# A two-block transformer on one core: triangle solved from a transposed copy, inverse decay by a second scan, squares summed by contiguous additions, 14 ring slots through the attentions

## The chip, the cores and the metric

One core of a Trainium2 chip runs the whole program. The metric is device time of one execution in microseconds. TensorE (PE in the profile) does matrix products, VectorE (DVE) and ScalarE (ACT) the elementwise work, GpSimd (POOL) little, and SyncE (SP) issues nearly all DMAs.

## The reference, cut to what matters

256 tokens of width 1024 go through two blocks, in float32.

```python
def first_block(x, mem, ...):                      # two layers
    for layer in range(2):
        att = (spatial gating if layer == 0 else dilated attention) + memory attention, projected
        x = layer_norm(ALPHA * x + att, ...)
        expert, gate = route(h, w_router, b_router)         # top 2 of 16 experts
        ffn = moe_ffn(h, expert, gate, w_gate, w_up, w_down)  # 16 x 3 matrices of 1024 x 1024
        x = layer_norm(ALPHA * x + ffn, ...)

def second_block(x, ...):                          # two layers
    for l in range(2):
        x = x + 0.5 * swiglu(rms_norm(x, norm_ffa[l]), ...)   # 1024 -> 2 x 2816 -> 1024
        x = x + hybrid_mixer(rms_norm(x, norm_mix[l]), ...)   # retention, sparse attention, rwkv7
        x = x + 0.5 * swiglu(rms_norm(x, norm_ffb[l]), ...)
    return rms_norm(x, norm_final)

def rms_norm(x, g):
    return x * rsqrt(mean(x * x, -1) + 1e-6) * g

def rwkv7_time_mix(...):                           # 8 heads of width 64, a state per head
    def step(S, inp):
        sa = einsum(S, -kk_t)
        S = S * w_t + sa * (kk_t * a_t) + v_t * k_t
        return S, einsum(S, r_t)
```

## The kernel before

**First block.** Weights come from HBM in tiles of 1 MB through a ring of slots in SBUF. In an attention (`attn_a`, `attn_b`) each unit of weights takes a ring slot (`raw_unit`), and ACT and DVE split it into a high and a low float32r part (`split_act`, L331 and L332, into the tiles `whi` and `wlo`), from which `mm3` makes three float32r matmuls for one float32 product (L100). A ring slot is free once its unit is split. The order of the DMAs on SP's queue is the program's; the expert weights of the following `moe` come right behind the last unit of the attention, so they begin to fill the ring while the attention still computes. In `moe` the eight pairs of experts each take 24 tiles (8 of `w_gate`, 8 of `w_up`, 8 of `w_down`), multiplied as plain float32 at L1870. `fetch` (issued at L1749) gives each tile a slot in turn: `slots = e.ring + 3` = 15, 12 of them in the ring and three in a pool `wst2` that exists in `moe` alone; tiles 11 to 15 have places of their own. From then on a fetch waits until TensorE has used what was in its slot. Before the sixth pair's third product there is a conditional branch (an overflow path, not taken), ahead of which `slots` tiles are fetched.

**Second block.** An FFN (`ffn`) streams weights in 512 KB tiles, split by ACT (L228) and DVE (L230), and does 11 column blocks of gate and up products with the down product of the block before in between. `rms_row` makes the factor of the norm: ACT squares x in two halves (L282), DVE sums each half over four strips of 256 with a reduction whose inner step is 256 elements (L283), adds the two (L284), a float32 matmul with ones sums over partitions (L286), then a root and a reciprocal (L289). It runs six times, within the first column block of an FFN or at the start of a mixer.

**Mixer.** The products of all branches are streams of L100 matmuls; the branches' own work is put between them by a priority. `rwkv_front` makes per group of two heads (`scaled`, four times) the decay: an exponential on ACT (L716), a running product over chunks of 32 by a scan on DVE (L718), and its inverse by a reciprocal (L721). `rwkv_back` then inverts the 128 unit triangles of 32 x 32 by forward substitution: they come back from DRAM into `LX`, one triangle in each partition, row by row; step t multiplies `X[:, :, :t+1]` by column t of the triangle (L811) and reduces (L812). The result goes through DRAM (`xscr`) into another layout, and the recurrence over chunks follows (`masks`, `solve`, `chunks`, `step`).

```python
    LXv = LX.rearrange("p (s t) -> p s t", s=32)
    for t in range(1, 32):
        nc.vector.tensor_mul(tmp, X[:, :, :t + 1], bc(LXv[:, :t + 1, t], 1, 16))
        nc.vector.tensor_reduce(X[:, :, t], tmp, axis=AX.X, op=OP.add)
```

`LXv[:, :t + 1, t]` is a column: its elements lie 32 floats (128 bytes) apart.

Of the kernel before, what the change touches and what calls it, by code (L numbers as in the profile page):

```python
# [111 lines left out]
def setup(ctx, tc, I, off):  # L112
    e = Env()
    e.tc, e.nc, e.I, e.off = tc, tc.nc, I, off
    nc = tc.nc
    P = lambda n, b, **k: ctx.enter_context(tc.tile_pool(name=n, bufs=b, **k))
    e.pool = P
    e.k = P("consts", 1)
    ident = e.k.tile([128, 128], F32, name="ident")
    nc.gpsimd.dma_start(ident, I["cst"][:, :128])  # L120
    e.c = {"ident": ident}
    e.ones = e.k.tile([128, 128], F32, name="ones")
    nc.vector.memset(e.ones, 1.0)
    e.eps = P("edge", 1, side="right").tile([128, 56], F32, name="eps")[:, :4]
    for i, v in enumerate((1e-6, 64e-5, 1e-5, -0.5 * E05)):
        nc.vector.memset(e.eps[:, i:i + 1], v)
    e.ahead, e.chain = 20000, 8000
    e.tail, e.first = (), None
    return e
# [145 lines left out]
def rms_row(e, cols=False, bank=None):  # L275

    nc = e.nc
    s1 = e.t1()
    part = [e.t1(), e.t1()]
    for i in range(2):  # L280
        sq = e.t4()
        nc.scalar.activation(sq.rearrange("p (k t) -> p k t", k=4), e.xT[:, 4 * i:4 * i + 4], AF.Square)  # L282
        nc.vector.tensor_reduce(part[i], sq.rearrange("p (k t) -> p t k", k=4), axis=AX.X, op=OP.add)  # L283
    nc.vector.tensor_add(s1, part[0], part[1])  # L284
    pb = (bank or e.bank)()
    nc.tensor.matmul(pb[:, :T], e.ones, s1, start=True, stop=True)  # L286
    rs = e.t1()
# [15 lines left out]
def turned(pool, n, name, o=TURN, tag=None):  # L303

    return pool.tile([128, n + 64], F32R, name=name, tag=tag or name)[:, o:o + n]


# [365 lines left out]
def rwkv_front(e, l, sub):  # L673
# [32 lines left out]
    def scaled(P):  # L706
# [9 lines left out]
        nc.scalar.activation(dsc[:, :, 1:33], c8(sig), AF.Exp, bias=e.eps[:, 3:4], scale=-0.5 * E05)  # L716
        W = e.t1(264).rearrange("p (c t) -> p c t", c=8)
        nc.vector.tensor_tensor_scan(W.rearrange("p c t -> p (c t)"), dsc.rearrange("p c t -> p (c t)"),  # L718
                                     e.c["scan1"], 0.0, OP.mult, OP.add)
        Wi = c8(sig)  # L720
        nc.vector.reciprocal(Wi, W[:, :, 1:33])  # L721
        WC = e.act.tile([128, 8], F32, name="WC", bufs=4)
# [71 lines left out]
def rwkv_back(e, l, front):  # L794
# [8 lines left out]
    for hf in range(2):  # L803
        nc.sync.dma_start(LX[hf * 64:(hf + 1) * 64], ltf)
    nc.vector.memset(LX[:, 0:1024:33], 1.0)
    LXv = LX.rearrange("p (s t) -> p s t", s=32)
    X = e.t2().rearrange("p (s t) -> p s t", s=16)
    nc.sync.dma_start(X, I["dec"][:, 2048:].rearrange("p (s t) -> p s t", s=16))
    for t in range(1, 32):
        tmp = e.t2().rearrange("p (s t) -> p s t", s=16)[:, :, :t + 1]  # L810
        nc.vector.tensor_mul(tmp, X[:, :, :t + 1], bc(LXv[:, :t + 1, t], 1, 16))  # L811
        nc.vector.tensor_reduce(X[:, :, t], tmp, axis=AX.X, op=OP.add)  # L812
# [269 lines left out]
def setup1(ctx, e):  # L1082
    nc = e.nc
    P = lambda n, b: ctx.enter_context(e.tc.tile_pool(name=n, bufs=b, reuse_waits="tile"))
    e.ring = 12
    e.wst = P("wst1", e.ring)
# [82 lines left out]

def split_unit(e, w, moving=False):  # L1170

    out = []
    for i in range(4):
        hi, lo = [turned(p, 512, n, 32 if moving else 0).rearrange("p (a b) -> p a b", a=2)
                  for p, n in ((e.whl, "whi"), (e.wlo, "wlo"))]
        split_act(e, w[:, 2 * i:2 * i + 2], hi, lo)
        out += [(hi[:, k], lo[:, k]) for k in range(2)]
    return out


def unit(e, src, moving=False):
    with e.tc.high_priority(offset=e.ahead):
        w = raw_unit(e, src.shape[1])
        load(e, w, src, 0, 1)
        return split_unit(e, w, moving)


def split_T(e, src, pool, wsrc):

    hh, hl = [turned(pool, KD * T, n).rearrange("p (k t) -> p k t", k=KD) for n in ("hh", "hl")]  # L1190
    sv = src.rearrange("(k p) t -> p k t", p=128)
# [164 lines left out]
def out_proj(e, w, parts):  # L1356
# [4 lines left out]
    for i, (k0, a) in enumerate(parts):  # L1361
# [6 lines left out]
        with e.tc.high_priority(offset=e.ahead):  # L1368
            w = raw_unit(e, 2)
            load(e, w, wv[:, k0:k0 + 2], 0, 1)  # L1370
            for j, n in jn:
                u[j, n] = [turned(p, 512, nm, 32) for p, nm in ((e.whl, "whi"), (e.wlo, "wlo"))]
                split_act(e, w[:, j, n * 512:(n + 1) * 512], *u[j, n])
# [13 lines left out]
def attn_a(e):  # L1387
# [17 lines left out]
    mem_keys(e, proj_T(e, u, mT))  # L1405
    nc.scalar.copy(e.mv, proj_N(e, unit(e, w8("w_mem_v", 0), True), mT))
    mp.close()
# [6 lines left out]
    for c in range(3):  # L1414
        pb = proj_N(e, unit(e, wv[:, :, 768 + c * 256:768 + (c + 1) * 256], True), hT)
        if c == 1:
# [50 lines left out]
def attn_b(e):  # L1467
# [17 lines left out]
    pool = hp.enter_context(e.tc.tile_pool(name="hT", bufs=1, side="right", reuse_waits="tile"))  # L1485
    hh, hl = [turned(pool, KD * T, n).rearrange("p (k t) -> p k t", k=KD) for n in ("hh", "hl")]

# [103 lines left out]
    for c in range(3):  # L1591
        sl = slice(c * 256, (c + 1) * 256)
        nc.scalar.copy(V[:, :, sl], proj_N(e, unit(e, wv[:, :, sl], True), hT))
    hp.close()
# [117 lines left out]
def moe(e, l, done, kv):  # L1712
# [11 lines left out]
    with ExitStack() as xs:  # L1724
        xT = xs.enter_context(tc.tile_pool(name="rx", bufs=1, reuse_waits="tile")).tile([128, KD, T], F32, name="xT")

        def evac(q, pt):
# [6 lines left out]
             for x in (2 * pr, 2 * pr + 1)]  # L1734
    loaded, turn, slots = {}, [0], e.ring + 3

# [47 lines left out]
    xg = []  # L1784
    wst2 = st.enter_context(tc.tile_pool(name="wst2", bufs=3, reuse_waits="tile"))
    ext = ExitStack()
# [356 lines left out]
```

## Time and profile before

| what | value |
|---|---|
| median of 3 runs | 2665.57 us (2660.73 to 2668.93) |
| the profiled execution | 2659.33 us, its span 2657.6 us |
| TensorE busy | 2555.9 us, 96% of the span |
| VectorE busy | 1372.1 us, 52% |
| ScalarE busy | 1017.5 us, 38% |
| HBM read | 684.48 MB, 259 GB/s over the span |

The span is the time from the first instruction to the last; 1.7 us of the execution lie around it. Busy time of TensorE is modelled, so a busy TensorE need not be at its full rate; the number of its matmuls in a stretch tells more. The first block takes about 1170 us, each FFN about 185, each mixer about 370.

### The profile page before, as it was taken

The page shows a single profiled execution, that of the slowest core. Times are in us where ns is not written, and L with a number is a line of the kernel's source. Part 1 is how long each engine was busy: PE and PEld are TensorE (multiplying, and loading weights), DVE is VectorE, ACT ScalarE, POOL GpSimd, SP SyncE. Part 2 cuts the span into 40 slices and gives each one's busy share as a digit, 9 for nine tenths or more (in the row PEclk, how much of TensorE's full clock was granted, in tenths as well). Part 3 has the DMA queues.
Part 4 walks back from the last instruction along what each step waited for, and adds up shares of the span by engine and source line. Part 5 has one row for each costly group of instructions (what it writes and reads, how often), then busy time and mean ns, then how long its engine had stood idle before and what let it go on. Part 6 is the DMA issues. An engine that isn't in the chain of part 4 may idle for free.

```text
span 2657.6 us, 43520 instructions
## 1 busy us (share of the span) xinstructions
PE 2555.9 (96%) x17866; PEld 1934.5 (73%) x17866; DVE 1372.1 (52%) x2204; ACT 1017.5 (38%) x1666; POOL 111.9 (4%) x175
## 2 busy tenths in 40 slices
PE   8999998999999998989999999999999999999998
PEld 7643433348643333359999988999999999889998
DVE  6521100027430100045578888776666788977755
ACT  7311100027311000044456564554454565645543
POOL 0000000000000000000000022000000000230000
PEclk9999999999999999999999999999999999999999
DMA  9799999996789999986656543566566565425663
GB/s 347 316 368 422 421 421 399 405 387 243 294 352 421 421 421 388 422 315 187 187 156 168 161 128 96 171 214 191 184 197 195 161 172 159 139 87 167 214 196 119
DMA packets 307204, 691.67 MB, mean 260 GB/s; under 512 B 26208, under 2 KB 229984, under 8 KB 259632
## 3 DMA queue, kind: packets, MB, share of 16 engines
q1 hardware_dynamic: 304976, 681.40, 71.5%
q0 software_dynamic: 976, 5.70, 0.6%
q8 instruction: 145, 2.38, 0.4%
q10 hardware_dynamic: 1040, 1.64, 0.2%
q14 instruction: 67, 0.55, 0.1%
HBM read 684.48 MB, written 4.19 MB: 259 GB/s over the span
## 4 chain that ended last, share of the span: by engine, by line
PE 47%; DMA 6%; DVE 6%; issue 1%; ACT 1%; SPq 0%; DVEq 0%; ACTq 0%
PE sbank L100 22%; PE ubank L100 9%; PE bank L100 9%; DVE wlo L230 2%; DMA w<-in_w_up_dram 2%; DMA w<-in_w_down_dram 1%; PE bank L1870 1%; PE abank L100 1%; DMA w<-in_w_gate_dram 1%; DVE t L811 1%; DMA w<-in_ffb_w_in_dram 1%; DVE t L812 0%; DMA w<-in_w_out_dram 0%; DMA w<-in_w_in_dram 0%; ACT whi L228 0%
## 5 line engine op out<-in xcount | busy, mean ns | idle before, releaser
L228 ACT CAST whi<-w 128x1024 fp32r<-128x1024 f32 x452 | 471.4, 1051 | 500.6 <-PE sbank L100 218.3
L230 DVE TENSOR_TENSOR wlo<-w,whi 128x1024 fp32r<-128x1024 f32 x452 | 552.4, 1227 | 82.8 <-PE sbank L100 27.3
L1870 PE MATMUL bank<-w,xg 128*64 128x512 f32 x1960 | 485.0, 598 | 19.1 <-DMA w<-in_w_up_dram 19.0
L100 PE MATMUL sbank<-hh,whi 128*128 128x256 f32 x1408 | 397.8, 283 | 8.3 <-ACT whi L331 6.1
L1870 PEld LDWEIGHTS bank<-w,xg 128*64 128x64 f32 x1960 | 165.1, 136 | 325.6 <-issue 259.4
L100 PE MATMUL sbank<-hh,wlo 128*128 128x256 f32 x1408 | 396.1, 282 | 4.2 <-DVE wlo L230 3.0
L100 PE MATMUL sbank<-hl,whi 128*128 128x256 f32 x1408 | 398.0, 283 | 2.1 <-DVE hl L324 1.7
L100 PEld LDWEIGHTS sbank<-hh,whi 128*128 128x128 f32 x1408 | 266.4, 189 | 12.3 <-ACT whi L331 6.6
L100 PEld LDWEIGHTS sbank<-hh,wlo 128*128 128x128 f32 x1408 | 266.5, 189 | 7.4 <-DVE wlo L230 3.8
L100 PEld LDWEIGHTS sbank<-hl,whi 128*128 128x128 f32 x1408 | 266.9, 190 | 6.3 <-issue 3.1
L1870 PE MATMUL bank<-w,aT 128*64 128x512 f32 x1024 | 247.5, 605 | 16.9 <-PEq L1963 12.4
L1870 PEld LDWEIGHTS bank<-w,aT 128*64 128x64 f32 x1024 | 84.9, 139 | 165.7 <-issue 149.2
L100 PE MATMUL ubank<-hh,wlo 128*128 128x256 f32 x704 | 195.5, 278 | 0.0
L100 PE MATMUL ubank<-hh,whi 128*128 128x256 f32 x704 | 195.3, 277 | 0.0
L100 PE MATMUL ubank<-hl,whi 128*128 128x256 f32 x704 | 195.2, 277 | 0.0
L100 PE MATMUL bank<-al,whi 128*128 128x256 f32 x704 | 189.5, 278 | 1.0 <-DVE al L332 1.0
L100 PE MATMUL bank<-ah,wlo 128*128 128x256 f32 x704 | 189.7, 277 | 0.0
L100 PE MATMUL sbank<-wlo,hh 128*128 128x256 f32 x624 | 178.4, 286 | 4.2 <-DVE wlo L230 3.5
L100 PE MATMUL sbank<-whi,hh 128*128 128x256 f32 x624 | 177.2, 285 | 0.6 <-ACT whi L331 0.6
L100 PE MATMUL sbank<-whi,hl 128*128 128x256 f32 x624 | 177.0, 284 | 0.0
L100 PE MATMUL bank<-ah,whi 128*128 128x256 f32 x704 | 175.3, 278 | 0.6 <-ACT ah L331 0.4
L1937 DVE TENSOR_TENSOR xn<-fbank,xn 128x512 f32<-128x512 f32 x60 | 41.4, 691 | 257.6 <-PE fbank L1935 257.6
(511 smaller groups left out, 4194.2 us busy)
## 6 DMA issues: line engine op xcount, KB each, us to landing
w<-in_w_gate_dram SPq DMA_DIRECT2D x128, 1024.0 KB, 19.8
w<-in_w_up_dram SPq DMA_DIRECT2D x117, 1024.0 KB, 19.8
w<-in_w_down_dram SPq DMA_DIRECT2D x112, 1024.0 KB, 19.8
w<-in_w_in_dram SPq DMA_DIRECT2D x140, 512.0 KB, 3.6
w<-in_ffa_w_in_dram SPq DMA_DIRECT2D x88, 512.0 KB, 4.7
w<-in_ffb_w_in_dram SPq DMA_DIRECT2D x88, 512.0 KB, 4.6
w<-in_ffa_w_out_dram SPq DMA_DIRECT2D x44, 512.0 KB, 4.3
w<-in_ffb_w_out_dram SPq DMA_DIRECT2D x44, 512.0 KB, 4.4
```

Source lines behind the costliest of these rows:

```text
L100: m = nc.tensor.matmul(out, a, b, start=first and i == 0, stop=last and i == 2, skip_group_check=skip)
L228: c = nc.scalar.copy(hi, w)
L230: m = nc.vector.tensor_sub(lo, w, hi.bitcast(F32))
L811: nc.vector.tensor_mul(tmp, X[:, :, :t + 1], bc(LXv[:, :t + 1, t], 1, 16))
L1870: m = nc.tensor.matmul(pb[n][64 * i:64 * i + 64], lhs(k, i), ws[i][j][:, sl], start=k == 0, stop=k == KD - 1, tile_position=(0, 64 * i))
L1937: nc.vector.tensor_add(yacc[t][:, sl], out, yacc[t][:, sl])
```

## The change

It does four things. The first: the ring has 14 slots; `wst2` has two instead of three, so that `moe` turns over 16 slots instead of 15. To make room in the attentions the tiles `whi` and `wlo` lose 256 bytes each (the offset of 128 bytes, for those that are a moving operand, with them), and the pair `hh`, `hl` becomes one tile. The second: ACT copies `LX` transposed into `LT`, and the substitution reads rows of `LT`, which are contiguous. The third: the inverse decay comes from a second exponential with the opposite sign and a second scan; the reciprocal goes. The fourth: `rms_row` adds the two squared halves and folds the sum twice, by additions of contiguous operands, splits it into two float32r parts and multiplies both with ones.

```diff
@@ rms_row
-    part = [e.t1(), e.t1()]
+    sq = [e.t4() for _ in range(2)]
     for i in range(2):
-        sq = e.t4()
-        nc.scalar.activation(sq.rearrange("p (k t) -> p k t", k=4), e.xT[:, 4 * i:4 * i + 4], AF.Square)
-        nc.vector.tensor_reduce(part[i], sq.rearrange("p (k t) -> p t k", k=4), axis=AX.X, op=OP.add)
-    nc.vector.tensor_add(s1, part[0], part[1])
+        nc.scalar.activation(sq[i].rearrange("p (k t) -> p k t", k=4), e.xT[:, 4 * i:4 * i + 4], AF.Square)
+    q = sq[0]
+    nc.vector.tensor_add(q, q, sq[1])
+    nc.vector.tensor_add(q[:, :512], q[:, :512], q[:, 512:])
+    nc.vector.tensor_add(s1, q[:, :256], q[:, 256:512])
+    parts = [e.s1.tile([128, 264], F32R, name="t1r", tag="t1")[:, :T] for _ in range(2)]
+    split_act(e, s1, *parts)
     pb = (bank or e.bank)()
-    nc.tensor.matmul(pb[:, :T], e.ones, s1, start=True, stop=True)
+    for i, q in enumerate(parts):
+        nc.tensor.matmul(pb[:, :T], e.ones.bitcast(F32R), q, start=i == 0, stop=i == 1)
@@ new
+def edge_h(pool):
+    h = pool.tile([128, 2 * KD * T + 16], F32R, name="h")[:, :2 * KD * T].rearrange("p (i k t) -> p i k t", i=2, k=KD)
+    return h[:, 0], h[:, 1]
@@ rwkv_front, scaled
-        W = e.t1(264).rearrange("p (c t) -> p c t", c=8)
-        nc.vector.tensor_tensor_scan(W..., dsc..., e.c["scan1"], 0.0, OP.mult, OP.add)
-        Wi = c8(sig)
-        nc.vector.reciprocal(Wi, W[:, :, 1:33])
+        W, V = [e.t1(264).rearrange("p (c t) -> p c t", c=8) for _ in range(2)]
+        flat = lambda q: q.rearrange("p c t -> p (c t)")
+        nc.vector.tensor_tensor_scan(flat(W), flat(dsc), e.c["scan1"], 0.0, OP.mult, OP.add)
+        nc.scalar.activation(dsc[:, :, 1:33], c8(sig), AF.Exp, bias=e.eps[:, 4:5], scale=0.5 * E05)
+        nc.vector.tensor_tensor_scan(flat(V), flat(dsc), e.c["scan1"], 0.0, OP.mult, OP.add)
+        Wi = V[:, :, 1:33]
@@ rwkv_back
-    nc.vector.memset(LX[:, 0:1024:33], 1.0)
-    LXv = LX.rearrange("p (s t) -> p s t", s=32)
+    LT = e.t4()
+    nc.scalar.copy(LT.rearrange("p (t s) -> p t s", t=32), LX.rearrange("p (s t) -> p t s", s=32))
+    nc.vector.memset(LT[:, 0:1024:33], 1.0)
+    LTv = LT.rearrange("p (t s) -> p t s", t=32)
-        nc.vector.tensor_mul(tmp, X[:, :, :t + 1], bc(LXv[:, :t + 1, t], 1, 16))
+        nc.vector.tensor_mul(tmp, X[:, :, :t + 1], bc(LTv[:, t, :t + 1], 1, 16))
@@ setup1, split_unit, out_proj, split_T, attn_b, moe
-    e.ring = 12
+    e.ring = 14
-        hi, lo = [turned(p, 512, n, 32 if moving else 0)...
+        hi, lo = [p.tile([128, 512], F32R, name=n)...
-    hh, hl = [turned(pool, KD * T, n).rearrange("p (k t) -> p k t", k=KD) for n in ("hh", "hl")]
+    hh, hl = edge_h(pool)
-    loaded, turn, slots = {}, [0], e.ring + 3
+    loaded, turn, slots = {}, [0], e.ring + 2
-    wst2 = st.enter_context(tc.tile_pool(name="wst2", bufs=3, reuse_waits="tile"))
+    wst2 = st.enter_context(tc.tile_pool(name="wst2", bufs=2, reuse_waits="tile"))
```

## Rows read from the trace of the kernel before

**Rows 1.** The page: engine's busy time, two costly groups, one DMA group.

```profile
PE 2555.9 (96%) x17866; PEld 1934.5 (73%) x17866; DVE 1372.1 (52%) x2204; ACT 1017.5 (38%) x1666; POOL 111.9 (4%) x175
...
L228 ACT CAST whi<-w 128x1024 fp32r<-128x1024 f32 x452 | 471.4, 1051 | 500.6 <-PE sbank L100 218.3
L230 DVE TENSOR_TENSOR wlo<-w,whi 128x1024 fp32r<-128x1024 f32 x452 | 552.4, 1227 | 82.8 <-PE sbank L100 27.3
...
w<-in_w_gate_dram SPq DMA_DIRECT2D x128, 1024.0 KB, 19.8
```

**Rows 2.** Windows, first `moe`: busy us (count) PE, PEld, DVE, ACT, POOL; clock; DMA; GB/s.

```profile
100.00:125.00 25.00, 20.72 (x115) 13.74 (x117) 13.58 (x50) 9.99 (x21) 4.28 (x4) 0.93 0.62 247
...
175.00:200.00 25.00, 25.00 (x110) 9.16 (x112) 3.70 (x6) 1.76 (x3) 0.00 (x0) 1.00 0.92 344
200.00:225.00 25.00, 24.89 (x118) 9.93 (x115) 3.86 (x6) 3.47 (x6) 0.00 (x0) 1.00 1.01 423
```

**Rows 3.** Waits of SP's queue, 115 to 210 us: total us, times, longest.

```profile
SPq L1749 <- PE bank L1870: 77.0, 26, 13.3
```

**Rows 4.** The chain that ended last, end of the second `moe`: start, us, what.

```profile
1099.28 19.79 DMA w<-in_w_gate_dram
...
1119.13 19.86 DMA w<-in_w_up_dram
```

**Rows 5.** Windows, triangle stage of mixer 0 (first two) and mixer 1.

```profile
1494.00:1520.00 26.00, 26.00 (x219) 25.80 (x220) 26.00 (x76) 12.80 (x18) 0.00 (x0) 1.00 0.64 183
...
1530.00:1565.00 35.00, 33.91 (x267) 29.75 (x266) 34.83 (x51) 24.44 (x55) 7.58 (x7) 1.00 0.46 128
...
2265.00:2300.00 35.00, 33.82 (x267) 29.75 (x267) 34.75 (x51) 24.01 (x55) 8.32 (x8) 1.00 0.46 127
```

**Rows 6.** Groups by line on DVE, 1480 to 1566 us: busy us, mean ns, idle.

```profile
L811 DVE TENSOR_TENSOR t<-t,t 128x32 f32<-128x32 f32 (+30 forms) x31 | 20.7, 667 | 0.2
L812 DVE TENSOR_REDUCE t<-t 128x16 f32<-128x32 f32 (+30 forms) x31 | 13.4, 433 | 0.2
```

**Rows 7.** The same by shape, 1480 to 1600 us.

```profile
L843 DVE TENSOR_TENSOR t<-gs,cst 128x512 f32<-128x512 f32 x4 | 2.7, 699 | 0.0
...
L840 DVE TENSOR_TENSOR t<-gs,cst 128x256 f32<-128x256 f32 x4 | 1.7, 442 | 0.0
...
L811 DVE TENSOR_TENSOR t<-t,t 128x512 f32<-128x512 f32 x1 | 1.1, 1136 | 0.0
```

**Rows 8.** Groups by line on DVE, 1410 to 1460 us (decays of mixer 0).

```profile
L721 DVE RECIPROCAL t<-t 128x256 f32<-128x256 f32 x4 | 7.0, 1744 | 0.0
L718 DVE TENSOR_TENSOR_SCAN t<-t,cst 128x264 f32<-128x264 f32 x3 | 2.1, 701 | 3.1 <-ACT t L716 3.1
```

**Rows 9.** One line's instructions, the exponential: ns min/median/max.

```profile
L716 ACT ACTIVATE t<-t,eps x8: 502/508/521, 1408.0 to 2187.2; 128x256 f32<-128x256 f32 x8
```

**Rows 10.** A tile's instructions, first norm, 1175 to 1192 us: ns min/median/max.

```profile
L283 DVE TENSOR_REDUCE t<-t x2: 1993/2005/2017, 1173.7 to 1182.0; 128x256 f32<-128x1024 f32 x2
...
L284 DVE TENSOR_TENSOR t<-t,t x1: 414/414/414, 1185.1 to 1185.1; 128x256 f32<-128x256 f32 x1
```

**Rows 11.** Timeline of PE around the first norm's matmul: start, us, what.

```profile
1186.51 0.28 PE L100 MATMUL sbank<-hh,whi 128*128 128x256 f32 x1
1186.62 0.28 PE L100 MATMUL sbank<-hl,whi 128*128 128x256 f32 x1
1186.73 0.59 PE L286 MATMUL ubank<-t,ones 128*128 128x256 f32 x2
...
1187.40 0.28 PE L100 MATMUL sbank<-hl,whi 128*128 128x256 f32 x1
1187.52 0.28 PE L100 MATMUL sbank<-hh,wlo 128*128 128x256 f32 x1
```

**Rows 12.** Windows of 150 us within the first FFN and the second.

```profile
1188.00:1338.00 150.00, 150.00 (x1276) 150.00 (x1275) 89.10 (x92) 66.79 (x73) 0.00 (x0) 1.00 0.61 187
1763.00:1913.00 150.00, 149.34 (x1315) 148.94 (x1314) 89.97 (x95) 66.93 (x76) 0.00 (x0) 1.00 0.62 194
```

More of the change, by code (lines that the diff above doesn't have):

```diff
@@ L123, in setup @@
     nc.vector.memset(e.ones, 1.0)
-    e.eps = P("edge", 1, side="right").tile([128, 56], F32, name="eps")[:, :4]
-    for i, v in enumerate((1e-6, 64e-5, 1e-5, -0.5 * E05)):
+    e.eps = P("edge", 1, side="right").tile([128, 56], F32, name="eps")[:, :5]
+    for i, v in enumerate((1e-6, 64e-5, 1e-5, -0.5 * E05, 0.5 * E05)):
         nc.vector.memset(e.eps[:, i:i + 1], v)
@@ L716, in scaled @@
         nc.scalar.activation(dsc[:, :, 1:33], c8(sig), AF.Exp, bias=e.eps[:, 3:4], scale=-0.5 * E05)
-        W = e.t1(264).rearrange("p (c t) -> p c t", c=8)
-        nc.vector.tensor_tensor_scan(W.rearrange("p c t -> p (c t)"), dsc.rearrange("p c t -> p (c t)"),
-                                     e.c["scan1"], 0.0, OP.mult, OP.add)
-        Wi = c8(sig)
-        nc.vector.reciprocal(Wi, W[:, :, 1:33])
+        W, V = [e.t1(264).rearrange("p (c t) -> p c t", c=8) for _ in range(2)]
[4 more added lines that the diff above has]
+        Wi = V[:, :, 1:33]
         WC = e.act.tile([128, 8], F32, name="WC", bufs=4)
@@ L1167, in raw_unit, with split_unit @@
     return e.wst.tile([128, 2048], F32, name="w").rearrange("p (a b) -> p a b", a=a)
-def split_unit(e, w, moving=False):
+def split_unit(e, w):
     out = []
     for i in range(4):
-        hi, lo = [turned(p, 512, n, 32 if moving else 0).rearrange("p (a b) -> p a b", a=2)
+        hi, lo = [p.tile([128, 512], F32R, name=n).rearrange("p (a b) -> p a b", a=2)
                   for p, n in ((e.whl, "whi"), (e.wlo, "wlo"))]
@@ L1178, in split_unit, with unit @@
     return out
-def unit(e, src, moving=False):
+def unit(e, src):
     with e.tc.high_priority(offset=e.ahead):
@@ L1184, in unit @@
         load(e, w, src, 0, 1)
-        return split_unit(e, w, moving)
+        return split_unit(e, w)
 def split_T(e, src, pool, wsrc):
-    hh, hl = [turned(pool, KD * T, n).rearrange("p (k t) -> p k t", k=KD) for n in ("hh", "hl")]
+    hh, hl = edge_h(pool)
     sv = src.rearrange("(k p) t -> p k t", p=128)
@@ L1371, in out_proj @@
             for j, n in jn:
-                u[j, n] = [turned(p, 512, nm, 32) for p, nm in ((e.whl, "whi"), (e.wlo, "wlo"))]
+                u[j, n] = [p.tile([128, 512], F32R, name=nm) for p, nm in ((e.whl, "whi"), (e.wlo, "wlo"))]
                 split_act(e, w[:, j, n * 512:(n + 1) * 512], *u[j, n])
@@ L1405, in attn_a @@
     mem_keys(e, proj_T(e, u, mT))
-    nc.scalar.copy(e.mv, proj_N(e, unit(e, w8("w_mem_v", 0), True), mT))
+    nc.scalar.copy(e.mv, proj_N(e, unit(e, w8("w_mem_v", 0)), mT))
     mp.close()
@@ L1414, in attn_a @@
     for c in range(3):
-        pb = proj_N(e, unit(e, wv[:, :, 768 + c * 256:768 + (c + 1) * 256], True), hT)
+        pb = proj_N(e, unit(e, wv[:, :, 768 + c * 256:768 + (c + 1) * 256]), hT)
         if c == 1:
@@ L1485, in attn_b @@
     pool = hp.enter_context(e.tc.tile_pool(name="hT", bufs=1, side="right", reuse_waits="tile"))
-    hh, hl = [turned(pool, KD * T, n).rearrange("p (k t) -> p k t", k=KD) for n in ("hh", "hl")]
+    hh, hl = edge_h(pool)
     def evac(q, pt):
@@ L1592, in attn_b @@
         sl = slice(c * 256, (c + 1) * 256)
-        nc.scalar.copy(V[:, :, sl], proj_N(e, unit(e, wv[:, :, sl], True), hT))
+        nc.scalar.copy(V[:, :, sl], proj_N(e, unit(e, wv[:, :, sl]), hT))
     hp.close()
```

## The prediction

> **What bounds the kernel now.** I read the page first. TensorE is busy for 96% of the span [rows 1], so an edit is worth only what it gives back to TensorE, or to whatever TensorE waits for. Since busy time there is modelled, the windows come next, with their counts.
>
> In the first block the windows show two regimes. At 200 to 225 us the DMAs move 423 GB/s [rows 2], and the page's slices hold about that rate for most of both `moe` stages: they end when the last byte comes. The chain agrees: at the end of the second `moe` it is DMA upon DMA [rows 4]. Before that, at 100 to 125 and 175 to 200 us, DMA runs at 247 and 344 GB/s with TensorE busy [rows 2]. The view of SP's waits names the reason: its fetches waited 77.0 us in total, from 115 to 210 us, for TensorE to use what was in their slots [rows 3]. So early in a `moe` the stream is held at a fixed distance ahead of TensorE, and from about 200 us on it runs flat out to the end of the layer. What counts is its lead when the hold ends.
>
> In the second block the FFNs are TensorE alone. The mixers are not: where the triangles are inverted (1485 to 1565 us in the first), VectorE is busy 26.00 us of 26 and 34.83 of 35 [rows 5]. TensorE looks busy there too, but starts 267 matmuls in 35 us, 7.6 a microsecond, against 1315 in 150, or 8.8, in an FFN [rows 5, 12]. It is fed too slowly by VectorE, which also makes the low parts of the weights.
>
> **The change part by part.** *Ring.* 16 slots instead of 15 let the stream be one tile further ahead when the hold ends. A tile costs what it takes at full rate: 1.0486 MB at 423 GB/s [rows 2] is 2.48 us (from issue to landing one takes 19.8 us [rows 1, 4], so eight share the way). The two slots more in the attention are worth nothing beyond that, because the hold after it comes later and sets the distance anew; both extra tiles are only fetched earlier. Two layers: -5.0 us. Bounds: 0, if the extra fetch is late behind another wait on SP's queue, and 2 x 2 x 2.48 = -9.9, if two tiles of lead survived. On SP's queue the fetch now issued before tiles 11 to 15 is a further one of `w_down`; those have 20 us until they are used, so nothing waits for them. The lost offsets in `whi`, `wlo` I cost at nothing: products from the same tiles start 0.11 or 0.12 us apart in one and the same product [rows 11], so no address sets that step. If the offset did matter, the bound is the difference of the two steps (0.0046 us, below) for the matmuls with a moving weight, 7 x 48 of single width and 6 x 24 of double width in both attentions, 624 widths, +2.9 us.
>
> *Triangle.* The 31 multiplications take 20.7 us [rows 6]. Their sizes are 16(t+1) elements, t from 1 to 31, 8432 in all. A contiguous product of 512 elements takes 699 ns and one of 256 takes 442 [rows 7]: 1.00 ns an element and 0.185 us each. So 31 x 0.185 + 8432 x 0.00100 = 14.2 us, against 1136 ns for 512 elements now [rows 7]; the reductions over the same shapes, 13.4 us [rows 6], say the same. VectorE: -6.5 us a mixer. Added at the head of the chain is one copy of 1024 elements on ScalarE, 1.05 us if its strided read costs what a contiguous cast does [rows 1], and twice that if it suffers as L811 does (1136 / 699 = 1.6 and more for the smaller share of fixed time). I take 1.05 us, as ScalarE has no row with such a penalty: -5.4 us. How much arrives? TensorE's deficit against the FFN rate is 40 matmuls in these 35 us (8.77 x 35 - 267), some 4.5 us at 0.113 each, and 9 in the 26 us before, 1.0 us [rows 5, 12]. Relief of 5.4 and deficit of 5.5 fit, so I take -5.0 us a mixer, -10.0 for both; the second one's window is like the first's [rows 5]. Bounds: 0, if TensorE's own order holds it there, and -2 x 6.5 = -13.
>
> The Trainium skill (Advanced Engine Details and Errata, SBUF Cachelines) says that SBUF has lines of 16 bytes and that touching a new line at every access costs a penalty. By that rule the ScalarE copy, which reads with steps of 128 bytes, pays it too. On VectorE the trace agrees (L811, 1136 ns against 699); no row here shows a ScalarE read of that kind. At 1.6 times, an estimate from those two rows, the copy is 0.6 us longer a mixer and the sum 1.2 us smaller.
>
> *Decay.* Four times a mixer, a reciprocal of 1744 ns goes and a scan of 701 comes on VectorE, -4.2 us in all, and ScalarE gets an exponential of 508 ns, +2.0 [rows 8, 9]. At 1410 to 1460 us the chain runs through TensorE's products without a break, and those cover it: worth 0. If that cover were gone, -8.4 for both mixers would be the end. The new wait: the second exponential overwrites what the first scan reads, so ScalarE waits for the scan, with the casts of weights (L228) queued behind it, and TensorE behind those.
>
> *Norm.* Per call VectorE loses two reductions of 2005 ns and an addition of 414 [rows 10], 4.42 us, and gets 1.227 (1024 elements [rows 1]), 0.699 (512), and two of 0.414, 2.75 in all; ScalarE gets a copy of 256 columns, at most the 0.51 of the exponential of that width [rows 9]. The latency after the second square is 2.4 us now and 3.3 then; products of the next column block hide either. The float32 matmul with ones, about 0.43 us on TensorE (1186.62 to 1187.40 holds it and three others [rows 11]: 0.78 less 3 x 0.117), becomes two of 0.115: -0.2 us, six times, -1.2. Bounds: 0 and -2.6.
>
> Sum: -5.0 - 10.0 - 0 - 1.2 = -16.2 us. Against the profiled execution, 2659.33, that is 2643.1; the median of the runs shown is 2665.57, 6.2 us above it, and as the timed runs are what is asked for I give 2665.57 - 16.2 = 2649.4, rounded to **2649 us**.
>
> **The rivals.** *Cadence.* Matmuls of the same kind start 0.113 us apart in the FFNs, or 0.118: in the first FFN 1276 fit in 150 us, in the second 1315, at a granted clock of 1.00 in both [rows 12]. The slower step begins right after the norm's float32 matmul: 0.11 before it, 0.12 after [rows 11], and lasts until the first FFN's end, some 1424 matmuls. With float32r in its place the step may stay short: 1424 x 0.0046 = -6.5 us more, 2643. Against it: the other FFNs contain the same float32 matmul and are quick but for short stretches, so it is not the sole cause.
>
> *The relief is swallowed.* VectorE is freed, but TensorE, whose order was fixed with other durations in mind, or the copy and ScalarE's queue ahead of it, becomes the bound of the triangle stage. Then only ring and norm remain, -6.2: 2659. For it: TensorE counts as busy there [rows 5]; against it: its count of matmuls.
>
> *Slower: the second exponential.* VectorE already waited 3.1 us for the first exponential, over three scans [rows 8], 1.0 us each. In `scaled` the two engines now wait for each other twice. If the added wait reaches TensorE through the casts, eight times, it eats the gain at 16.2 / 8 = 2.0 us each, and ends beyond 0.3% slower from 24.2 / 8 = 3.0 us on. At 3.5 us each the time is 2665.57 - 16.2 + 28 = 2677. Against: VectorE has slack in that stage, and the casts run ahead of their products.
>
> *No gain from the ring*, because the fetches of the added slots wait for pools of the attention at new addresses: 2654, which stays in the forecast's range.
>
> **How the numbers follow.** A measurement of this kernel tells 0.3%, or 8 us, from no change: the three runs spread over 8.2. Chances: the forecast (2644 to 2655) 0.43; cadence (2637 to 2644) 0.24; relief swallowed (2655 to 2664) 0.19; slower by more than 8 us 0.08; other cases near no change 0.06. The first two are faster by over 0.3% (below 2657.6), and of the swallowed case a quarter: 0.72. Slower 0.08; the rest, 0.20, is within. For 8 in 10 the range takes the forecast, the cadence case down to 2637 and the swallowed case up to 2663; what is left out is slower, or has several bounds at their ends at once.
>
> **What would show it.** In the profile after: 31 multiplications at about 14 us instead of 20.7, and windows of the triangle stage with more matmuls per microsecond; a copy before them of 1.05 us, or near 1.7; a start of the FFN after the second `moe` some 5 us earlier, with the hold at 115 to 210 us still there; `rms_row`'s chain hidden; the count of matmuls in the first FFN's window 1276 again, or 1315. The prediction is wrong if TensorE's deficit in the mixers moves to a later stage instead of shrinking, if ScalarE's waits for scans reach TensorE, or if the cadence changes in several FFNs, each worth some 6 us either way.

## The result, and the profile after

The changed kernel takes 2638.33 us (median of 6 runs, 2635.18 to 2649.40) against 2666.48 of the kernel before (6 runs, 2660.73 to 2668.93): ratio 0.9892, 95% interval 0.9871 to 0.9913, so 28.8 us less by the ratio. A second series gave 2644.87 and 0.9913 (0.9881 to 0.9944). The kernel is faster, as forecast, and 2638.33 lies within 2637 to 2663, but only 1.3 us above the lower end: the gain is larger than the -16.2 us of the sum. The profiled execution took 2637.24 us with a span of 2635.5, 22.1 less than the span before.

Where the 22.1 us came from is read from the timeline of TensorE: the time up to the matmul of the first norm (`rms_row`), then from each norm's matmul to the next norm's, and from the last to the end of the span.

| stretch (us) | start to norm 1 | first FFN | mixer 0 | FFN | FFN | mixer 1 | last FFN |
|---|---|---|---|---|---|---|---|
| before | 1186.7 | 188.6 | 368.0 | 183.6 | 183.0 | 367.3 | 180.3 |
| after | 1184.7 | 182.3 | 360.1 | 183.5 | 183.6 | 361.7 | 179.7 |
| difference | -2.0 | -6.3 | -7.9 | -0.1 | +0.6 | -5.6 | -0.6 |

*Ring.* The first fence is the group of the expert products, after, and the second the same group before: shortest, median and longest duration in ns, then first and last start. The last product of the second `moe` starts 2.6 us earlier. The hold is still there: SP's queue waited for TensorE just as in [rows 3] (third fence, 115 to 210 us, after).

```profile
L1883 PE MATMUL bank<-w,xg x1960: 592/592/644, 116.9 to 1139.5; 128*64 128x512 f32 x196
```

```profile
L1870 PE MATMUL bank<-w,xg x1960: 592/592/644, 116.6 to 1142.1; 128*64 128x512 f32 x196
```

```profile
SPq L1762 <- PE bank L1883: 77.0, 26, 13.3
```

*Triangle.* The first fence has the groups on DVE from 1465 to 1552 us, after: 31 multiplications take 14.2 us, as worked out (20.7 in [rows 6]); the reductions are unchanged. By shape the largest takes 691 ns against 1136 [rows 7].

```profile
L824 DVE TENSOR_TENSOR t<-t,t 128x32 f32<-128x32 f32 (+30 forms) x31 | 14.2, 458 | 0.3
L825 DVE TENSOR_REDUCE t<-t 128x16 f32<-128x32 f32 (+30 forms) x31 | 13.5, 436 | 0.1
```

```profile
L824 DVE TENSOR_TENSOR t<-t,t 128x512 f32<-128x512 f32 x1 | 0.7, 691 | 0.0
```

The next fence is the copy's line, after, once in each of the two mixers: 2.08 us each, twice the 1.05 of the sum, at the head of the chain.

```profile
L817 ACT COPY t<-t x2: 2075/2084/2092, 1470.1 to 2197.1; 128x1024 f32<-128x1024 f32 x2
its engine sat idle before it (us, times) until:
  DMA t<-lscr: 5.3, 2
who waited for it (us, times):
  DVE t L818: 8.1, 2
```

The windows of the triangle stage, after, that answer to [rows 5], moved with the stage: 230 matmuls start in 26 us instead of 219, and 282 and 279 in 35 us instead of 267 and 267. VectorE is no longer full in the latter two (31.79 and 31.57 us of 35). In the first window it is as full as before, and the timeline has another reason for the 11 matmuls more: 194 of the 218 times between starts there were 116 to 119 ns before, and 220 of 227 are 110 to 115 after. What that is follows below.

```profile
1481.00:1507.00 26.00, 26.00 (x230) 25.90 (x229) 26.00 (x76) 14.02 (x24) 0.00 (x0) 1.00 0.70 197
1517.00:1552.00 35.00, 34.94 (x282) 31.07 (x281) 31.79 (x51) 27.43 (x60) 8.40 (x9) 1.00 0.48 132
2243.00:2278.00 35.00, 35.00 (x279) 31.03 (x278) 31.57 (x53) 27.28 (x59) 7.58 (x8) 1.00 0.50 140
```

*Decay.* The first fence has groups on DVE from 1398 to 1448 us, after. The second scans (L731) take 0.7 us where the reciprocals took 1.7 [rows 8]. The new wait exists, but is short: in both mixers together ScalarE waited 2.5 us for a scan before the second exponential, four times of eight (second fence, that line's instructions).

```profile
L731 DVE TENSOR_TENSOR_SCAN t<-t,cst 128x264 f32<-128x264 f32 x4 | 2.8, 702 | 0.4 <-ACT t L730 0.4
L729 DVE TENSOR_TENSOR_SCAN t<-t,cst 128x264 f32<-128x264 f32 x4 | 2.8, 701 | 2.9 <-ACT t L726 2.9
```

```profile
L730 ACT ACTIVATE t<-t,eps x8: 509/511/512, 1401.4 to 2169.0; 128x256 f32<-128x256 f32 x8
its engine sat idle before it (us, times) until:
  DVE t L729: 2.5, 4
```

*Norm and step.* Below, "short step" and "long step" are the times between starts of back-to-back 256-column float32r matmuls, 113 and 118 ns, and a long FFN is one with most of its steps long (about 6 us more than the 180 to 184 of the others). The fence has windows of 150 us in the first FFN and the second, after: 1319 matmuls where [rows 12] has 1276, and 1315 as before. The first FFN runs at the short step now: 43 matmuls more in 150 us, at a granted clock of 1.00 in both.

```profile
1188.00:1338.00 150.00, 149.51 (x1319) 149.32 (x1318) 91.91 (x97) 69.65 (x77) 0.00 (x0) 1.00 0.61 190
1745.00:1895.00 150.00, 149.34 (x1315) 148.94 (x1314) 89.91 (x92) 66.23 (x75) 0.00 (x0) 1.00 0.62 193
```

### The profile page after: what moved, and what is told of

Read it like the earlier page. It is cut to its first block, busy times and chain, and to the rows that moved or that the text cites. A ratio compares the mean times of both kernels' runs of the same rounds, so it can differ in the third digit from the quotient of the medians.

```text
span 2635.5 us, 43540 instructions
## 1 busy us (share of the span) xinstructions
PE 2543.6 (97%) x17866; PEld 1927.6 (73%) x17866; DVE 1345.0 (51%) x2211; ACT 1029.5 (39%) x1686; POOL 107.4 (4%) x175
## 4 chain that ended last, share of the span: by engine, by line
PE 49%; DMA 5%; DVE 4%; ACT 2%; issue 1%; SPq 0%; DVEq 0%; ACTq 0%
PE sbank L100 23%; PE ubank L100 9%; PE bank L100 9%; PE bank L1883 2%; DVE wlo L230 2%; DMA w<-in_w_up_dram 2%; PE abank L100 1%; DMA w<-in_w_gate_dram 1%; DMA w<-in_w_down_dram 1%; DMA w<-in_w_in_dram 1%; DMA w<-in_ffb_w_in_dram 1%; ACT whi L228 0%; DMA w<-in_w_out_dram 0%; DMA t<-lscr 0%; PE bank L720 0%
## 5 line engine op out<-in xcount | busy, mean ns | idle before, releaser
L1883 PE MATMUL bank<-w,xg 128*64 128x512 f32 x1960 | 483.5, 597 | 17.1 <-DMA w<-in_w_up_dram 16.9
L100 PE MATMUL sbank<-hh,wlo 128*128 128x256 f32 x1216 | 340.9, 281 | 3.4 <-DVE wlo L230 3.4
L100 PE MATMUL sbank<-hh,whi 128*128 128x256 f32 x1216 | 341.0, 281 | 1.0 <-ACT hh L333 0.9
L100 PE MATMUL sbank<-hl,whi 128*128 128x256 f32 x1216 | 339.5, 279 | 1.7 <-DVE hl L334 1.7
L100 PEld LDWEIGHTS sbank<-hh,wlo 128*128 128x128 f32 x1216 | 229.2, 189 | 6.2 <-DVE wlo L230 4.8
L100 PEld LDWEIGHTS sbank<-hh,whi 128*128 128x128 f32 x1216 | 229.2, 188 | 4.2 <-issue 2.3
L100 PEld LDWEIGHTS sbank<-hl,whi 128*128 128x128 f32 x1216 | 229.3, 189 | 3.8 <-DVE hl L334 1.9
L100 PE MATMUL bank<-al,whi 128*128 128x256 f32 x704 | 189.0, 277 | 1.0 <-DVE al L342 1.0
L100 PE MATMUL bank<-ah,wlo 128*128 128x256 f32 x704 | 189.0, 276 | 0.0
L100 PE MATMUL sbank<-wlo,hh 128*128 128x256 f32 x512 | 144.9, 283 | 0.1
L100 PE MATMUL sbank<-whi,hl 128*128 128x256 f32 x512 | 144.9, 283 | 0.0
L100 PE MATMUL sbank<-whi,hh 128*128 128x256 f32 x512 | 143.5, 282 | 0.0
```

Of the source, the lines that this page charges most:

```text
L100: m = nc.tensor.matmul(out, a, b, start=first and i == 0, stop=last and i == 2, skip_group_check=skip)
L1883: m = nc.tensor.matmul(pb[n][64 * i:64 * i + 64], lhs(k, i), ws[i][j][:, sl], start=k == 0, stop=k == KD - 1, tile_position=(0, 64 * i))
```

## The experiments

Twelve runs followed, in six series; each ratio is to the kernel before on the same chip.

**The four parts one by one**, each alone in the kernel before. The diffs are those of the change.

> The kernel before with the triangle's part alone (transposed copy, rows instead of columns). The forecast's step says -10.0 us (ratio 0.9962), about -5 in each mixer, and the 31 multiplications at about 14 us a mixer instead of 20.7. The rival that the relief is swallowed says within 2 us of the kernel before. If the mixers' gain comes from the decay instead, this run shows -5 us or less. The first FFN keeps its 1276 matmuls in the window of 150 us if the norm's float32 matmul is what makes its step slow; if the slow step is an accident of one execution, it may show 1315 or more here.

> The kernel before with the second scan alone. The forecast's step says 0 us, since TensorE's products cover the decay. The rival that the cover is partly gone says up to -8.4 us (ratio 0.9968), seen as an earlier start of the triangle stage in both mixers. The rival of the second exponential says slower, 2 to 3 us for each of the eight uses, +16 us or more.

> The kernel before with the norm's part alone (contiguous additions, two float32r matmuls). The forecast's step says -1.2 us. The cadence rival says -1.2 - 6.5 = -7.7 us (ratio 0.9971), with a count of 1315 or more matmuls in the first FFN's window of 150 us instead of 1276.

> The kernel before with the ring's part alone (14 slots and two in moe, no offsets in whi and wlo). The forecast's step says -5.0 us (ratio 0.9981), 2.5 at the end of each moe. The rival from the first look at the trace after says -2.6 us at the end of the second moe, and nothing more behind it. The first FFN keeps 1276 matmuls in its window if the float32 matmul makes the step slow.

| part alone | ratio (95% interval) | us at 2666.5 |
|---|---|---|
| triangle | 0.9952 (0.9935 to 0.9969) | -12.8 |
| second scan | 0.9997 (0.9981 to 1.0012) | -0.8 |
| norm | 1.0001 (0.9984 to 1.0018) | +0.3 |
| ring | 0.9970 (0.9956 to 0.9983) | -8.0 |

The triangle and the ring carry the gain; both forecasts (-10.0 and -5.0) lie in the intervals. The scan is worth nothing that can be measured: neither the 16 us more of one rival nor the 8.4 less of the other. The norm alone does not show the cadence rival's -7.7. The four add up to -21.3, each with an interval of some 4 us to either side; the whole gave -28.8 (-34.4 to -23.2) and -23.2 (-31.7 to -14.9), so the sum is not told apart from either.

Mixer 0 as one window (norm to norm), for the kernel before, the triangle alone, the scan alone and the whole change: the same 3115 to 3117 matmuls in 368.0, 365.0, 368.7 and 360.0 us.

```profile
1375.40:1743.40 368.00, 356.35 (x3117) 330.96 (x3116) 306.86 (x568) 213.68 (x398) 46.29 (x68) 1.00 0.52 152
```

```profile
1378.00:1743.00 365.00, 356.10 (x3117) 331.89 (x3117) 301.90 (x568) 214.87 (x399) 43.09 (x68) 1.00 0.52 153
```

```profile
1374.40:1743.10 368.70, 360.07 (x3116) 334.15 (x3115) 303.99 (x568) 218.73 (x404) 46.96 (x68) 0.99 0.52 152
```

```profile
1367.00:1727.00 360.00, 352.49 (x3115) 328.09 (x3114) 296.52 (x569) 220.41 (x406) 44.03 (x68) 1.00 0.53 154
```

The sign that the scan's expectation named for its rival did come: with the scan alone the first multiplication of the triangle stage starts 102.9 us after the mixer's norm instead of 110.2 (below, its group in mixer 0, before and with the scan alone). But the gain did not: 932 matmuls start ahead of it instead of 991, those left over run behind it, and the mixer takes 368.7 us against 368.0.

```profile
L811 DVE TENSOR_TENSOR t<-t,t x31: 195/664/1291, 1485.6 to 1561.2; 128x32 f32<-128x32 f32 x1, 128x48 f32<-128x48 f32 x1, 128x64 f32<-128x64 f32 x1, 128x80 f32<-128x80 f32 x1
```

```profile
L812 DVE TENSOR_TENSOR t<-t,t x31: 195/668/1509, 1477.2 to 1555.6; 128x32 f32<-128x32 f32 x1, 128x48 f32<-128x48 f32 x1, 128x64 f32<-128x64 f32 x1, 128x80 f32<-128x80 f32 x1
```

The surprise is in the FFNs of these profiles. Long ones (bold), in us from norm to norm:

| kernel | first | second | third | last |
|---|---|---|---|---|
| before | **188.6** | 183.6 | 183.0 | 180.3 |
| triangle alone | **189.0** | **189.5** | 182.9 | 179.9 |
| scan alone | **188.7** | **189.4** | 183.2 | 179.7 |
| norm alone | 186.0 | 183.5 | **188.9** | **186.2** |
| ring alone | 182.7 | **189.5** | 182.9 | 180.4 |

The ring alone, with the float32 matmul in place, has a quick first FFN; the norm alone, without it, has two long ones. So the long step is no property of one FFN, and the float32 matmul is not its only source.

The norm alone's first FFN has short steps; its 186.0, against 182.3 in the changed kernel, comes from waits. In its order of instructions 17 other matmuls stand between the two of the first norm's pair, 4 in the changed kernel. ScalarE waits 1.42 us for the pair before it can take the root, and TensorE then waits 2.0 and 1.2 us for the splits of the first column block, which need the norm's factor (below, its waits from 1180 to 1380 us; the changed kernel has none at this place). So the norm's latency is not hidden in every order, and what the part alone shows is its shorter step less these waits.

```profile
PE bank L100 <- ACT ah L335: 2.0, 1, 2.0
PE bank L100 <- DVE al L336: 1.6, 2, 1.2
```

**The whole once more, its norm, and the ring taken apart.** The edits, each alone:

```diff
 e6: the changed kernel, rms_row
-    parts = [...]; split_act(e, s1, *parts)
-    for i, q in enumerate(parts): nc.tensor.matmul(pb[:, :T], e.ones.bitcast(F32R), q, ...)
+    nc.tensor.matmul(pb[:, :T], e.ones, s1, start=True, stop=True)
 e7: the kernel before                       e8: the changed kernel
-    slots = e.ring + 3, wst2 bufs=3        -    slots = e.ring + 2, wst2 bufs=2
+    slots = e.ring + 4, wst2 bufs=4        +    slots = e.ring + 1, wst2 bufs=1
```

> The changed kernel once more, unaltered, for a second profile and a closer time beside the kernels of this call. The single parts gave -8.0, -12.8, -0.8 and +0.3 us, -21.3 in all, against -28.2 for the whole. If the sum holds this gives about -22 us (ratio 0.992) and in its profile one or two FFNs at the slow step (188 to 190 us from norm to norm instead of 183), as in the kernels before. If the whole change really keeps the FFNs at the short step, it gives -28 us again (0.989) and all four FFNs at 180 to 184 us.

> The changed kernel with the norm's float32 matmul back (the contiguous additions stay, the split and the two float32r matmuls go). The forecast's step says +1.2 us on the changed kernel. The cadence rival, in the form that this matmul turns the step to the slow one wherever it stands and that only a later stall of TensorE turns it back: +6 us for each FFN that no stall rescues, and in the profile the slow step begins directly behind each of the six matmuls. If the step is a matter of chance alone, 0.

> The kernel before with a fourth slot in the pool that exists in moe alone: 16 slots there, 12 in the attentions as before. The forecast's step says the whole gain of the ring, -5.0 us (2.5 at the end of each moe), is here, since what counts is the distance within moe. The rival, that it is the two more slots through the attentions (weights waiting ready when an attention or a moe starts), says 0 here.

> The changed kernel with one slot less in the pool of moe: 14 slots in the attentions, 15 in moe. The forecast's step says +5.0 us on the changed kernel, 2.5 at the end of each moe. The rival that the attention's slots carry the gain says 0 on the changed kernel.

| kernel | ratio (95% interval) | us at 2666.5 | FFNs (long ones bold) |
|---|---|---|---|
| changed kernel again | 0.9913 (0.9881 to 0.9944) | -23.2 | 182.3, 183.5, 182.9, **185.9** |
| with the float32 matmul | 0.9936 (0.9910 to 0.9962) | -17.1 | **187.9**, 182.8, **188.4**, **185.9** |
| before, 16 slots in `moe` | 0.9971 (0.9951 to 0.9991) | -7.7 | 181.8, 184.0, **188.9**, 180.1 |
| after, 15 slots in `moe` | 0.9950 (0.9930 to 0.9969) | -13.3 | **192.6**, 183.5, 182.9, **185.9** |

*The ring:* 16 slots in `moe` and 12 in the attentions give -7.7, as much as the whole ring part (-8.0): the two slots through the attentions add nothing that can be seen. With 15 slots the changed kernel loses 9.9 us by the two ratios (the intervals overlap), but not all of that is the ring's: its order has the 17 matmuls within the first norm's pair too, its first FFN waits 3.1 us for the same splits, and it takes 192.6 us against 182.3. Its last expert product starts 3.1 us later than in the changed kernel's second profile (1140.5 against 1137.4). Over all profiles with the full program the last expert product starts at 1142.1, 1144.3, 1140.8, 1141.7 and 1140.5 us with 15 slots (mean 1141.9), and at 1139.5, 1135.0, 1137.4, 1136.9, 1136.3, 1137.1 and 1136.7 with 16 (mean 1137.0): -4.9 us. The first fence is of the kernel before with 16 slots, the second of the changed one with 15; in the former SP's queue is held as before, 81.7 us in 115 to 210 us (third fence).

```profile
L1870 PE MATMUL bank<-w,xg x1960: 592/592/644, 115.8 to 1136.3; 128*64 128x512 f32 x196
```

```profile
L1883 PE MATMUL bank<-w,xg x1960: 592/592/1113, 116.5 to 1140.5; 128*64 128x512 f32 x196
```

```profile
SPq L1749 <- PE bank L1870: 81.7, 27, 13.3
```

*The norm:* by the time the pair of float32r matmuls may be worth 6 us, but the intervals overlap too far to say. The profiles say more. Windows of 130 us in the first FFN and the last, of the changed kernel's second profile, and (second fence) the first and the third with the float32 matmul back: 1149 or 1106 to 1107 matmuls where no wait falls into the window.

```profile
1195.00:1325.00 130.00, 130.00 (x1149) 130.00 (x1148) 77.28 (x79) 58.17 (x64) 0.00 (x0) 1.00 0.62 190
...
2490.00:2620.00 130.00, 130.00 (x1107) 130.00 (x1106) 76.01 (x77) 56.93 (x63) 0.00 (x0) 1.00 0.56 171
```

```profile
1195.00:1325.00 130.00, 130.00 (x1106) 130.00 (x1106) 73.12 (x75) 55.23 (x60) 0.00 (x0) 1.00 0.61 187
...
1945.00:2075.00 130.00, 130.00 (x1106) 130.00 (x1105) 75.85 (x78) 56.49 (x62) 0.00 (x0) 1.00 0.60 186
```

I then followed the step through every norm but the last of each program, in the timelines of all twelve profiles that hold norms (these ten and the last two below). Directly behind the float32 matmul it was long 29 times of 30, in 21 of them after a short one. Behind the pair it went to the short one within a dozen matmuls, or up to the next wait, 30 times of 30. At the last norm both mostly left it as it was: the float32 matmul six times of six, five of them at the short step, the pair five times of six. Whether it stays so hangs on the next waits of TensorE: in the second FFN of the kernel before a step of 156 ns among steps of 118 was followed by 113 for over 1300 matmuls; in the third FFN of the norm alone one of 284 ns among steps of 113 was followed by as many at 118.

**The step by itself.** A stream of matmuls without the rest of the kernel.

```diff
+ for r in range(6):
+     for f in (pair, wait for 1 copy, wait for 2, wait for 4, transpose, 128 columns):
+         float32 matmul with ones;  72 matmuls (mm3);  f;  72 matmuls (mm3)
```

> No part of the reference is computed here: one unbroken stream of the three float32r matmuls of 256 columns from tiles that lie ready in SBUF, with nothing else running, in pieces of 72. Before every piece stands one of these: the norm's float32 matmul with ones; the pair of float32r matmuls that replaces it; a wait of TensorE for one, two or four copies on ScalarE; a float32 transpose; a float32r matmul of 128 columns. Each stands there six times, the float32 matmul 36 times. If the float32 matmul turns the step to the slow one, all 36 pieces behind it start at 118 ns, and those behind the pair stay as they were. If a wait draws the step anew, the pieces behind waits show both steps. If the step has nothing to do with what stands ahead, or comes from the other engines' traffic, all pieces show 113 ns.

All pieces ran at 120 ns whatever stood ahead, except right behind the longest waits: the question about the float32 matmul stayed open, and a third step had come up. The tiles lay differently here: the activations, which move through TensorE, and the weights, which stand in it, started at the same place modulo 128 bytes. So the next run has one more edit: padding that shifts the moving tiles by 64 bytes against the stationary ones, as they lie in the FFNs.

> The stream of the run before with one difference: the moving tiles lie 64 bytes further on against the stationary ones, as they do in the FFNs (in the run before both started at the same place within 128 bytes, and all pieces ran at 120 ns). If the place sets the step, pieces at 113 ns appear here. If then the float32 matmul turns the step to 118 ns, all pieces behind it show 118 and none 113; if a wait can turn it back, pieces behind the waits of one or two copies show 113, and those behind the pair of float32r matmuls stay as the piece before them. If the place has nothing to do with it, all pieces are at 120 ns again.

Now the pieces ran at 113 or 118 ns, none at 120. (The two streams ran on different chips; on the one of the stream without padding the FFNs of the last two runs below show 113 and 118 ns.) The first fence has windows of 8 us in pieces of the padded stream: behind the pair after a short piece, behind a float32 matmul, a wait for one copy, and 128 columns. The second and third have the same 78 us at the start of the padded stream, at the long step, and of the stream without padding:

```profile
109.00:117.00 8.00, 8.00 (x73) 8.00 (x72) 0.00 (x0) 0.00 (x0) 0.00 (x0) 1.00 0.01 2
117.60:125.60 8.00, 8.00 (x71) 8.00 (x70) 0.00 (x0) 0.00 (x0) 0.00 (x0) 1.00 0.00 0
127.00:135.00 8.00, 8.00 (x70) 8.00 (x69) 0.00 (x0) 0.00 (x0) 0.00 (x0) 1.00 0.01 2
...
199.50:207.50 8.00, 8.00 (x73) 8.00 (x72) 0.00 (x0) 0.00 (x0) 0.00 (x0) 1.00 0.00 0
```

```profile
20.00:98.00 78.00, 78.00 (x664) 78.00 (x664) 0.00 (x0) 0.00 (x0) 0.00 (x0) 1.00 0.01 1
```

```profile
20.00:98.00 78.00, 78.00 (x653) 78.00 (x652) 0.00 (x0) 0.00 (x0) 0.00 (x0) 1.00 0.00 1
```

| ahead of the piece (padded stream) | after a short step | after a long step |
|---|---|---|
| float32 matmul | 23 of 23 long | 7 short, 6 long |
| pair of float32r matmuls | 1 of 1 short | 5 of 5 short |
| wait of 0.74 us (one copy) | | 6 of 6 long |
| wait of 1.2 us (two) | 6 of 6 short | |
| wait of 2.05 us (four) | | 3 short, 3 long |
| float32 transpose | | 3 short, 3 long |
| float32r, 128 columns | | 6 of 6 short |

So traffic of other engines is not needed for it: with the tiles laid like this TensorE repeats one of two steps until something shifts it. In this stream the float32 matmul took it out of the short one each time, and the pair put it there each time; the last norms above show that the first does not hold everywhere. The three waits of four copies that left a short step are the three behind which the granted clock was at the lower of its two levels, 1.2 GHz.

**Two attempts to keep the FFNs at the short step**, in the changed kernel. Both add matmuls whose result is overwritten by the product that follows.

```diff
 def proj_T, ahead of the up product
+    e11, blocks 1, 2, 3, 6, 9: nc.tensor.matmul(pb[:, 0, :128], u[0][0][...], h[0][...][:, :128], ...)
+    e12, blocks 1, 3: for i, q in enumerate(h): nc.tensor.matmul(pb[:, 0], e.ones.bitcast(F32R), col(q, 0), ...)
```

> The changed kernel with one float32r matmul of 128 columns more (its result is overwritten by the product that follows) ahead of the up product of column blocks 1, 2, 3, 6 and 9 of each FFN, 20 in all, 0.06 us each, 1.2 us together. In the stream by itself such a matmul turned the slow step to the quick one six times of six; what it does to the quick step was not seen there. If the step is all that the FFNs' times differ by, and the short matmul leaves the quick step alone: all four FFNs at 181 to 184 us from norm to norm, none at 186 to 193, and about 5 us less than the changed kernel (1 or 2 slow FFNs of four at 6.3 us, less 1.2): ratio about 0.988. If the short matmul also turns the quick step to the slow one, several FFNs are slow and the time is that of the changed kernel or up to 15 us more.

> The changed kernel with a pair of float32r matmuls of 256 columns with ones (result overwritten by the product that follows) ahead of the up product of column blocks 1 and 3 of each FFN, eight pairs, 0.23 us each, 1.8 us together. In the stream by itself and at the norms of the runs before, such a pair left the quick step quick and turned the slow one to the quick one, but for the last norm. If the step is what FFNs differ by: all four FFNs at 181 to 184 us from norm to norm, in the timed runs too, so about 6 us less than the changed kernel (1.25 slow FFNs of four at 6.3 us, less 1.8): ratio 0.987 to 0.990. If waits behind the pairs draw the step anew all the same, the time is that of the changed kernel, with FFNs of 186 to 190 us among the four.

Neither beats the changed kernel: 0.9939 (0.9919 to 0.9959) and 0.9933 (0.9918 to 0.9948). The short matmul turns the step both ways: of 20, one met a wait, 11 stood behind short steps and left long ones, 8 the reverse. The FFNs alternate, about half their steps are long (186.2, 191.0, 187.3 and 185.0 us), and the six times spread over 5.0 us only (2651.03 to 2656.01; the changed kernel's over 14.2 and 17.6). Windows of 14 us of its second FFN: in block 1 behind a short matmul, in block 2 behind the next, in block 3 behind the third.

```profile
1735.00:1749.00 14.00, 14.00 (x121) 14.00 (x120) 11.61 (x14) 8.31 (x11) 0.00 (x0) 1.00 0.62 189
1752.00:1766.00 14.00, 14.00 (x126) 14.00 (x125) 8.38 (x9) 7.18 (x8) 0.00 (x0) 1.00 0.59 188
1770.00:1784.00 14.00, 14.00 (x122) 14.00 (x121) 8.15 (x9) 6.32 (x7) 0.00 (x0) 1.00 0.59 184
```

With the pairs the first and the last FFN are quick (182.3, 181.8), the third nearly so (184.8), but the second takes 195.0: the step turned long between the pairs, the second pair left it there, and at the FFN's end TensorE waited 2.7 us for a split (first fence, its waits from 1720 to 1920 us; 0.4 in the changed kernel). Behind that the granted clock was at the lower of its two levels, 1.2 GHz, for 6.8 us: 0.91 on the mean of the window in the second fence.

```profile
PE bank L100 <- ACT ah L345: 2.7, 1, 2.7
```

```profile
1884.00:1920.00 36.00, 33.15 (x261) 32.65 (x260) 23.86 (x31) 17.61 (x24) 0.00 (x0) 0.91 0.55 168
```

## Why the prediction held, and where its sum was short

*Ring, -5.0.* Right in mechanism and size: -8.0 alone (-11.7 to -4.5), -7.7 with the slots in `moe` alone, -4.9 by the traces. One tile of lead for each layer is what survives; the hold resets the rest, and the attention's slots are worth nothing, as argued. The profiled execution shows 2.6 only; the lists above, 3.8 and 4.5 us wide, show differences of that size between profiles with the same number of slots. The offsets lost in `whi` and `wlo` cost nothing that can be seen, but the reason given, that no address sets the step, was wrong: the two streams differ by 64 bytes of address and by 120 against 113 or 118 ns. An offset of 128 bytes, as the one removed, leaves the place within 128 as it was.

*Triangle, -10.0.* Right: -12.8 alone (-17.3 to -8.3), multiplications at 14.2 us as worked out. The copy was mis-sized: it took 2.08 us, the doubled price that the sum named and set aside, not 1.05. The Trainium skill (Advanced Engine Details and Errata, SBUF Cachelines) says that reaching a new line of SBUF at every access is penalised. The copy agrees: at 2.0 times the contiguous cast its penalty is larger than the 1.6 of VectorE. Relief of 4.4 us a mixer, not 5.4, met the deficit. The deficit itself was partly misread: of the 9 matmuls missing in the 26 us window most were missing by the long step and not by VectorE. In the two windows of 35 us the count rose by 15 and 12. Over all profiles both mixers together take 723.4 us on average in the six with contiguous rows and second scan, 727.0 with the triangle alone, and 737.2 in the five with columns; their long steps, 416 more on average in the last, are 1.9 of the 13.8 us between first and last. That leaves some -11.9 for triangle and scan, inside the bound of -13.

*Decay, 0.* Right in the sum (-0.8, -5.1 to +3.2), though the triangle stage did move. The wait of the second exponential is there and reaches nobody: the rival of the slower kernel falls.

*Norm, -1.2.* In the interval of the part alone (-4.3 to +4.8), which tells no more. What it does to VectorE is hidden in the changed kernel, but not in the norm alone and with 15 slots, where TensorE waited 3.2 and 3.1 us for it. What counts is the other thing it does.

*The step that failed* is that the cadence was left out of the sum, as a rival with a chance of 0.24 and one FFN. Both series lie in that rival's range, 2637 to 2644 (the second at 2642 by its ratio), and not in the forecast's own from 2644 up. That the first lies inside the whole range, by 1.3 us, is in part luck: one long FFN more or less is 6 us. In the profiled pair the rival came true nearly to the number: the first FFN, -6.3 us against -6.5 worked out. It also runs through the mixers, which the rival did not count: their long steps fell from 1117 and 1061 to 536 and 793, and 849 x 0.0046 us is -3.9 of the -13.5 us there. That leaves -9.6 for the triangle, if nothing else moved there. So -2.0 (ring here), -9.6 and -6.3 - 3.9 (step) make -21.8 of the 22.1. The objection held against the rival, that other FFNs have the same matmul and are quick, is explained: there a later wait turned the step back, or, in the last FFN, the matmul left the step short. The prediction had named a cadence that changes in several FFNs as a sign of being wrong; over the runs it does.

How much of the 28.8 the step gives on average is not settled. The programs with the float32 matmul showed 10 long FFNs of 24, those with the pair in its place 5 of 16; the changed kernel 0 and 1 of four. Chance alone could make that difference. At 6.3 us each, 10/24 against 5/16 of four is 2.6 us, and in their mixers they differ by 535 long steps on average, 2.5 us; the norm alone gave +0.3. By these averages the ring's -4.9, the triangle and scan's -11.9 and the step's -2.6 and -2.5 make some -22, which the second series (-23.2) fits and the first (-28.8) passes. What the profiles show is that the matmul sets the step behind it; what the step is an FFN later hangs on waits that no edit here held fixed. Whether the whole exceeds the parts' sum by chance or by an interplay was not tested. One interplay is seen: the order of instructions changes with the parts, and the norm alone has 3.2 us of waits that the whole has not.

*Relief swallowed* falls with the triangle's own run; *no gain from the ring* with both ring runs.

## What to carry to other kernels

Where a ring's stream is held by its consumer and then runs flat out, count what one more slot leaves as lead when the hold ends, per layer, and put it where the hold is. A strided column read by 31 operations is worth one transposed copy, even at twice a copy's price, when its engine is the full one. Before a difference of 0.2% between two profiles is put down to an edit, count the matmuls in a stretch that neither edit touches: here each such stretch is 6 us longer or not, by what happened ahead of it.

## What the runs showed of the hardware that I had not expected

- Back-to-back 256-column float32r matmuls, each with its own weights, at a granted clock of 1.00: 113 or 118 ns apart when moving and stationary tiles started 64 bytes apart modulo 128, 120 ns when they started at the same place (one layout of each was run as a stream by itself). The two steps persist for an FFN's length (1149 or 1106 matmuls in 130 us without a wait) until a wait or a matmul of another kind shifts them; a 128-column matmul turned them 19 times of 19 in the FFNs.
- ScalarE's copy that reads with a stride of 128 bytes took 2.08 us for 1024 columns, a contiguous cast 1.05.
- Behind the waits of 2.05 us the stream's steps were 213 ns for a while, TensorE at the lower of its two levels, 1.2 GHz, in six cases of six without padding and three of six with it (the window below, without padding, holds both levels and has a granted clock of 0.90). Behind waits of 0.74 and 1.2 us they were not.

```profile
171.00:178.00 7.00, 7.00 (x55) 7.00 (x54) 0.00 (x0) 0.00 (x0) 0.00 (x0) 0.90 0.00 0
```
